# A bidirectional encoder layer with two kinds of attention: 512-column matmuls in the tail, a first attention in blocks of 32 queries, and row sums regrouped by transposes

## The chip, the cores and the metric

The kernel runs on one core of one Trainium2 chip. The metric is the device time of one execution in microseconds (us); lower is better. All times below are of this core.

## The reference

One encoder layer is applied to two sequences of 2048 tokens and 1024 features, with shared weights. All data is float32.

```
h = rms_norm(x, norm_w)
q_a, k_a, v_a, g_a, q_b, k_b, v_b, g_b = split(h @ w_in)     # 512 128 128 512 512 512 512 512
o_a = windowed_gqa_sink(rope(norm(q_a)), rope(norm(k_a)), v_a, sink) * silu(g_a)
o_b = neighbourhood_attn(norm(q_b), norm(k_b), v_b, rpb) * silu(g_b)
x   = x + concat(o_a, o_b) @ w_out
out = x + (p @ w_ple) * sigmoid(x @ w_ple_gate)
```

The first attention (A) has 8 query heads of 64 features on 2 key heads; a token sees the tokens up to 128 away on both sides, and each head has a learned sink in its softmax's denominator. The second attention (B) has 8 heads; the tokens form a grid of 32 rows by 64 columns, and a token sees 8 rows by 16 columns around it, with a learned bias per relative position.

## The kernel before

Every matrix product is made in split precision: an operand is split into a high part (a rounded copy, made on ScalarE) and a low part (the rest, made on VectorE or GpSimd), and three matmuls, high x high, low x high and high x low, add up in PSUM. That is why a matmul appears in threes.

The order of all work is written by a planner in the kernel itself (class `Flow`). Each operation is given an engine, a planned duration, what it depends on, a priority, and the buffers that it takes and frees. `Flow.run` plays the engines through in planned time and emits, on each engine, the ready operation with the lowest priority number. On the chip every engine then runs its own list strictly in that order; a planned duration that is too short shows up as a wait there. All loads and stores are issued by one queue, SyncE's (SP), also in that order. Low-priority projections (`low`, 1000 and up) fill TensorE's time between the attention's steps.

**First attention.** `proj_a` takes 32 tiles of 128 tokens: keys and values in 24 matmuls of 256 columns, queries in 24 of 512, then norms and rotation. `prep_q` transposes a tile's queries and splits them; `unit_a` does the attention for a tile and one key head: `softmax` makes four score blocks, each of 128 queries of one head against 384 keys (256 at a sequence's ends) in two matmuls; VectorE adds the mask and takes the maximum, ScalarE does the exponential, GpSimd divides; twelve transposes, then six matmuls of 512 columns with the values.

**Row regrouping.** B uses the tokens in another order (tiles of 8 rows by 16 columns), so the mean squares of the rows must move from one order to the other. `regroup` runs once per sequence, when its last tile is projected: it writes 2048 values from a tile of 128 partitions by 16 columns to DRAM, each value by itself, writes the roots likewise, and reads the values back in the new order with 16 small loads, one per column.

**Second attention.** 64 steps: two halves of four heads, each of 2 sequences x 16 tiles. `proj_b` makes a tile's queries and keys (24 matmuls of 512 columns) and values (24 of 256, with ScalarE and VectorE writing the split values that are stored to DRAM by window), seven steps ahead of `unit_b`, which does the tile's attention. Beside that, `combine` makes sums of weight blocks on GpSimd for the tail, and after the last projection `embed` makes p @ w_ple in 384 matmuls of 512 columns.

**The tail.** Three stages of products with a 1024 x 1024 weight: the gate paths, the output projection, and the last gate. Each is done by a seven-product (Strassen-Winograd) scheme: per group of 512 tokens, taken as two halves of 256, `operand` builds seven moving operands from the group's quarters by additions and splits them; `product` multiplies each with a 512 x 512 weight set (`a11 a12 s2 s1 s3 a22 s4`), 48 matmuls of 256 columns, into two PSUM banks; `result` evicts a bank when it holds a partial or a final result, with the stage's gate or residual step (VectorE, ScalarE, GpSimd) and its side inputs. Sums of two result blocks share a bank over several products, so some products wait until an earlier result has been read. All seven weight sets of a stage stay in SBUF; the next stage's are loaded and split while the last group runs. Everything the tail needs beyond the first weights takes memory that is given free when the attention's pool (`ab_stack`) is closed, after the last step of B.

All instructions that go through the `Ordered` wrapper appear at line 210 of the profile; the matmuls of projections and attention at line 268, transposes at 271, the tail's matmuls at 1066.

## Time and profile before

| | us |
|---|---|
| median of 3 runs | 2729.1 |
| lowest, highest | 2724.32, 2730.3 |
| the profiled execution | 2731.31 |
| its span, first to last instruction | 2729.5 |

| engine | busy, us | share of the span |
|---|---|---|
| TensorE matmuls (PE) | 2567.4 | 94% |
| TensorE weight loads (PEld) | 2313.6 | 85% |
| VectorE (DVE) | 1949.8 | 71% |
| ScalarE (ACT) | 1549.6 | 57% |
| GpSimd (POOL) | 1462.6 | 54% |

The mean granted TensorE clock is 0.983 of full speed. Matmuls are pipelined: one of 256 columns is shown as busy for 0.28 us while the next begins before it ends, so a busy share near 100% does not say how many matmuls go through. The count of matmuls in a stretch does. A wait is put down to the engine whose signal came last. In a row of a group, the figures behind the bar are busy time, the mean of one in ns, and the idle time of the engine just before these instructions.

### The profile page before, as it was taken

How to read it: one execution, taken by the hardware profiler on the slowest of the kernel's cores; microseconds unless marked ns; L12 is line 12 of the kernel's file. 1: busy time of each engine (PE TensorE's matmuls, PEld its weight loads, DVE VectorE, ACT ScalarE, POOL GpSimd, SP SyncE). 2: the span in 40 equal slices, each digit the busy share in tenths (PEclk: the TensorE clock that was granted, in tenths of full speed). 3: DMA queues.
4: the chain of work that ended last, by engine and by line, in shares of the span. 5: the costliest groups of instructions: out<-in, count | busy, mean ns of one | idle time of the engine just before them, and what ended most of it. 6: DMA issues, size and time to landing. Idle time of an engine off the chain costs nothing. (4 is left out here: it accounts for less than half of the span.)

```text
span 2729.5 us, 49655 instructions
## 1 busy us (share of the span) xinstructions
PE 2567.4 (94%) x17264; PEld 2313.6 (85%) x17264; DVE 1949.8 (71%) x4054; ACT 1549.6 (57%) x3449; POOL 1462.6 (54%) x1517
## 2 busy tenths in 40 slices
PE   7999799989999999999999999899998999999999
PEld 6888688878787877787788777799988999999999
DVE  6888688977777667766767732988888554677775
ACT  6888588867676667766667765433333111243333
POOL 5666466655555554565555532567664232246654
PEclk9999899999999999999999999999999999999999
DMA  4534353335666667667666677555456544654453
GB/s 143 182 106 128 81 158 117 98 76 150 214 215 205 196 202 225 203 203 218 203 208 210 208 250 235 166 180 160 155 171 209 194 161 147 196 172 140 151 177 105
DMA packets 319466, 472.01 MB, mean 173 GB/s; under 512 B 72784, under 2 KB 178384, under 8 KB 309712
## 3 DMA queue, kind: packets, MB, share of 16 engines
q1 hardware_dynamic: 319216, 468.85, 55.2%
q8 instruction: 136, 2.23, 0.4%
q14 instruction: 114, 0.93, 0.1%
HBM read 321.91 MB, written 145.78 MB: 171 GB/s over the span
## 5 line engine op out<-in xcount | busy, mean ns | idle before, releaser
L268 PE MATMUL bank<-wa,xr 128*128 128x256 f32 (+1 forms) x2304 | 413.3, 326 | 14.2 <-DVE mx L210 11.4
L210 POOL TENSOR_SCALAR s<-s,rd 128x384 f32<-128x384 f32 (+4 forms) x512 | 291.1, 587 | 250.9 <-DVE rd L210 118.6
L268 PE MATMUL bank<-wb,xr 128*128 128x512 f32 x1536 | 405.4, 401 | 2.0 <-DVE big L210 1.6
L210 POOL TENSOR_TENSOR xr<-st,xr 128x512 fp32r<-128x512 f32 x208 | 268.2, 1291 | 216.9 <-ACT xr L210 200.1
L268 PEld LDWEIGHTS bank<-wa,xr 128*128 128x128 f32 x2304 | 337.9, 192 | 49.7 <-DVE mx L210 15.8
L210 ACT ACTIVATE s<-s,nm 128x384 f32<-128x384 f32 (+4 forms) x512 | 307.2, 602 | 81.3 <-DVE nm L210 79.3
L268 PEld LDWEIGHTS bank<-wb,xr 128*128 128x128 f32 x1536 | 274.8, 190 | 49.3 <-DVE big L210 1.8
L1066 PE MATMUL bank<-xr,s 128*128 128x256 f32 x2304 | 287.0, 285 | 15.2 <-DVE s L210 10.8
L1066 PEld LDWEIGHTS bank<-xr,s 128*128 128x128 f32 x2304 | 282.5, 194 | 17.0 <-issue 7.7
L210 DVE TENSOR_TENSOR p_t<-bank,p_t 128x512 fp32r<-128x512 f32 (+3 forms) x440 | 263.0, 624 | 41.5 <-ACT p_t L210 38.8
L268 PE MATMUL bank<-big,q 128*128 128x384 f32 (+4 forms) x1024 | 253.3, 355 | 22.3 <-DVE mx L210 8.4
L210 POOL TENSOR_TENSOR y<-vr,half_neg 128x8 f32<-128x8 f32 (+1 forms) x128 | 186.6, 1458 | 136.1 <-DVE vr L210 124.7
L210 ACT CAST p_t<-bank 128x512 fp32r<-128x512 f32 (+3 forms) x440 | 223.9, 541 | 53.5 <-PE bank L271 44.0
L210 DVE TENSOR_TENSOR s<-bank,s 128x512 f32<-128x512 f32 x208 | 142.5, 686 | 146.5 <-PE bank L1066 145.0
L271 PE MATMUL bank<-ident,s 128*128 128x128 f32 (+2 forms) x1568 | 225.1, 277 | 16.9 <-DVE big L210 7.1
L271 PEld LDWEIGHTS bank<-ident,s 128*128 128x128 f32 (+2 forms) x1568 | 181.5, 140 | 50.9 <-issue 13.0
L268 PEld LDWEIGHTS bank<-big,q 128*128 128x128 f32 x1024 | 165.5, 189 | 63.4 <-DVE mx L210 19.1
L210 DVE SCALAR_TENSOR_TENSOR big<-bank,wk,big 64x128 fp32r<-64x128 f32 x320 | 137.6, 430 | 110.2 <-ACT big L210 103.0
L210 DVE TENSOR_TENSOR ot<-bank,ot 64x256 f32<-64x256 f32 (+1 forms) x256 | 141.7, 553 | 85.9 <-ACT ot L210 81.4
L1066 PE MATMUL bank<-xr,wb 128*128 128x256 f32 x1584 | 195.8, 284 | 3.6 <-ACT xr L210 2.8
L1066 PEld LDWEIGHTS bank<-xr,wb 128*128 128x128 f32 x1584 | 193.3, 193 | 4.2 <-ACT xr L210 3.2
L210 ACT COPY ot<-bank 64x256 f32<-64x256 f32 (+1 forms) x256 | 121.4, 474 | 125.5 <-PE bank L268 98.8
(124 smaller groups left out, 5224.5 us busy)
## 6 DMA issues: line engine op xcount, KB each, us to landing
st<-x_b SPq DMA_DIRECT2D x128, 256.0 KB
vw<-v_d SPq DMA_DIRECT2D x107, 256.0 KB
st<-x_a SPq DMA_DIRECT2D x64, 256.0 KB
st<-x_n SPq DMA_DIRECT2D x64, 256.0 KB
v_d<-sq SPq DMA_DIRECT2D x64, 256.0 KB
ple_d<-raw SPq DMA_DIRECT2D x64, 256.0 KB
raw<-x_r SPq DMA_DIRECT2D x16, 1024.0 KB
og_d<-s SPq DMA_DIRECT2D x64, 256.0 KB
```

What stands on the lines that cost most here:

```text
L210: return lambda *a, **k: self.tc.keep_in_program_order(f(*a, **k))
L268: pinned(nc.tensor.matmul(out, lhsT, rhs, start=start, stop=stop))
L271: pinned(nc.tensor.transpose(out, in_, ident))
L1066: pinned(nc.tensor.matmul(ps, w[k][:, x, c:c + 128], o[:, y, k], start=new and kk == 0 and k == 0 and j == 0, stop=k == 3 and j == 2, skip ...
```

## The change

- **Tail.** Groups of 1024 tokens, in two halves of 512. A matmul has 512 columns; a product is 48 of them into four banks. There are 12 groups instead of 24. Operand additions and splits act on 2048 columns instead of 1024, results keep their 512. The fifth product's weight set (`s3`) and the second's (`a12`) share four tiles, so both are loaded and split again in every group. Side inputs go through two tiles.
- **Memory.** Pools are no longer closed; single tiles pass from one use to the next at three points: when the last projection is done, when the embedding is done, when the attention is done.
- **First attention.** A score block has 32 queries of each of the four heads of a key head, against the 288 keys that these can see (fewer at a sequence's ends), instead of 128 queries of one head against 384. The columns outside are set to zero once. Each of the four blocks has its own two tiles. The sink becomes one value per partition, which saves one small VectorE step.
- **Row regrouping.** The values and the roots of a sequence are transposed on TensorE into 32 rows, written to DRAM as rows of 128 values, read back in four loads, put in order by a VectorE copy and transposed back.
- **Second attention.** The values of both halves are projected in the first half, in 24 matmuls of 512 columns per tile, and evicted in two steps. At the beginning and at the turn of the halves, two tiles' query and key projections go ahead of their value projections.
- **Projections** are planned in pieces of two blocks of 128 features (six matmuls) instead of one. The first weights are loaded through four tiles instead of nine. The embedding's results go to tiles that come free with the last projection.

The core of the diff:

```diff
-TW = 256
-NU = SEQ // TW
+NU = 8
...
-    s_pool = pool(SB, [128, 512], F32, "s", mid)
-    p_pool = pool(3, [128, 2, 512], F32R, "p_t", mid, True)
-    x_pool = pool(2, [128, 2, KT, 128], F32R, "xr", mid, True)
-    st_pool = pool(2, [128, 512], F32, "st", mid, True)
-    big = [ap.tile([128, 4096], F32R, tag=f"big{i}", name=f"big{i}") for i in range(3)]
+    s_tiles = [new([128, 512], F32, f"s{i}") for i in range(SB)]
+    s_pool = Pool(s_tiles[8:])
+    s_block = [Pool(s_tiles[2 * b:2 * b + 2]) for b in range(4)]
...
+    first_pool = Pool(qa_pool.tiles)
+    ev_pool = Pool([])
...
+        parts = []
+        for b in range(4):
+            c0, c1 = max(32 * b, 128 * (k0 - t + 1)), min(32 * b + 288, 128 * (k1 - t + 1))
+
+            def sc(bank, b=b, c0=c0, n=c1 - c0):
+                c = 128 * (t - 1) + c0
+                for j, w in enumerate((hi[kv](), q2.t[:, kv])):
+                    mm(bank.t[:, :n], w[:, 128 * b:128 * b + 128], ks_a[:, kv, c:c + n], j == 0, j == 1)
+            parts.append((c1 - c0, sc, lambda b=b, c0=c0, c1=c1: mask[:, c0 - 32 * b:c1 - 32 * b], Slot(s_block[b]), c0))
...
-        vb, vops = project(f, "pv", 256, 120, xs, xdone, w_v, v_done, low(prios[1]), free=[xs])
+        after_pe[f] = (ops[-1], ops[-1])
+        if half:
+            return
+        vb, vops = project(f, "pv", 512, 231, xs, xdone, w_v, v_done, low(prios[1]), free=[xs], chunk=CH)
...
+        for hf in range(2):
+            sv = Slot(sq_pool)
+            v4 = lambda sv=sv: sv.t.bitcast(F32R).rearrange("p (h a d) -> p h a d", a=2, d=HD)
+            vp = lambda hf=hf: vb.t[:, 256 * hf:256 * hf + 256].rearrange("p (h d) -> p h d", d=HD)
+            vpr = pr + 0.1 + 0.2 * hf
...
-        l0 = dma(ms_d[s * SEQ:(s + 1) * SEQ].rearrange("(t p) -> p t", p=128), ms_a[:, c], 8, [root_ops[f] for f in range(NT * s, NT * s + NT)], pr)
-        dma(hr_d[s * SEQ:(s + 1) * SEQ].rearrange("(t p) -> p t", p=128), hr_a[:, c], 8, [root_ops[f] for f in range(NT * s, NT * s + NT)], pr)
-        rows = ms_d.rearrange("(r k c) -> r k c", k=4, c=16)
-        ls = [dma(ms_b[:, i:i + 1], rows[8 * (i // 4):8 * (i // 4) + 8, i % 4, :].rearrange("r c -> c r"), 8, [l0], pr)
-              for i in range(NT * s, NT * s + NT)]
+        bank, back = Slot(banks), Slot(banks)
+        own = [root_ops[f] for f in range(NT * s, NT * s + NT)]
+        t1 = op("PE", 110, lambda: tr(bank.t[:32, :128], mh_a[:, s].rearrange("p a t -> p (a t)")), own, pr, take=[bank])
+        c1 = op("DVE", 150, lambda: V.tensor_copy(out=mt[:32], in_=bank.t[:32, :128]), [t1, *(regrouped[-1:])], pr, free=[bank])
+        l0 = dma(ms_d[s * SEQ:(s + 1) * SEQ].rearrange("(t p) -> t p", p=128), mt[:NT], 8, [c1], pr)
+        l1 = dma(hr_d[s * SEQ:(s + 1) * SEQ].rearrange("(t p) -> t p", p=128), mt[NT:2 * NT], 8, [c1], pr)
+        rows = ms_d[s * SEQ:(s + 1) * SEQ].rearrange("(b r k c) -> b k r c", r=8, k=4, c=16)
+        ls = [dma(mt[4 * b:4 * b + 4].rearrange("k (r c) -> k r c", c=16), rows[b], 8, [l0, l1], pr) for b in range(4)]
+        c2 = op("DVE", 150, lambda: V.tensor_copy(out=mt[32:32 + NT].rearrange("p (c r) -> p c r", r=8),
+                                                  in_=mt[:NT].rearrange("p (r c) -> p c r", c=16)), ls, pr)
+        t2 = op("PE", 110, lambda: pinned(nc.tensor.transpose(back.t[:, :NT], mt[32:32 + NT], ident[32:32 + NT, 32:32 + NT])), [c2], pr, take=[back])
...
-        slot, n = Slot(s_pool), len(parts)
+        slot, n = Slot(first_pool), len(parts)
...
+    w_v, v_done = load_wide(wa, rows_of(w_in_c, 512), True, HB - 9, [after_pe[HB - 1], *ci])
...
+    order = {f: (2 * f, 2 * f + 1) for f in range(HB, 3 * HB)}
+    for f in (HB, 2 * HB - 2):
+        order[f], order[f + 1] = (2 * f, 2 * f + 2), (2 * f + 1, 2 * f + 3)
...
+    sets = {"a11": wa[4:], "a12": wa[:4], "s3": wa[:4]}
+    for i, name in enumerate(("s2", "s1")):
+        sets[name] = [big[i][:, 1024 * j:1024 * j + 1024].rearrange("p (a c) -> p a c", a=2) for j in range(4)]
...
+    def no_projections():
+        for j in range(4, 8):
+            t = new([128, 2, 512], F32R, f"wb{j}", f"vx{j}")
+            give(vw_pool, [t[:, 0], t[:, 1]])
+        for j in range(2):
+            t = new([128, 2, 512], F32, f"wb{j}", f"ev{j}")
+            give(ev_pool, [t[:, 0], t[:, 1]])
+
+    def no_embeddings():
+        sets["s4"] = [new([128, 2, 512], F32R, f"wb{j}", f"s4{j}") for j in range(4)]
+        give(od_pool, [t.rearrange("p a k t -> p (a k t)") for t in x_pool.tiles])
+        give(side_pool, st_pool.tiles)
+
+    def no_attention():
+        sets["a22"] = [new([128, 2, 512], F32R, f"wb{j}", f"a22{j}") for j in range(4, 8)]
+        p2 = new([128, 6, 512], F32, "p_t", "p2")
+        v2 = new([128, 5, 512], F32, "vw", "v2")
+        q3, q4 = new([128, 2048], F32, "q1", "q3"), new([128, 2048], F32, "q2", "q4")
+        o2 = new([128, 2, 2048], F32R, "big2", "o2")
+        give(raw_pool, [q3, q4, p2[:, :4].rearrange(f2), v2[:, :4].rearrange(f2)])
+        give(sum_pool, [misc.rearrange(f2), qb_all.rearrange("p a b c -> p (a b c)")])
+        give(th_pool, [p2[:, 4], p2[:, 5]])
+        give(s_pool, [v2[:, 4]])
+        give(root_pool, sq_pool.tiles)
+        give(od_pool, [o2[:, 0], o2[:, 1]])
...
+    load_q(0, "a11", PR - 13, [after_pe[f][1] for f in (2 * HB - 2, 2 * HB - 1)])
+    for name, gate, pr in (("a12", emb_end, -3), ("s2", att_end, -2), ("s1", att_end, -1), ("a22", att_end, 0), ("s4", emb_end, 1)):
+        load_q(0, name, T0 + pr, [gate])
+    groups = [(stage, g) for stage in range(3) for g in range(4)]
...
+            def go(st=st, mp=mp):
+                w, c = sets[name], 128 * mp
+                o = [x.t.rearrange("p (k t) -> p k t", k=4) for x in (hi, lo)]
+                for k in range(4):
+                    for j, (x, y) in enumerate(((0, 0), (1, 0), (0, 1))):
+                        pinned(nc.tensor.matmul(st[0].t, w[k][:, x, c:c + 128], o[y][:, k], start=first and k == 0 and j == 0,
+                                                stop=k == 3 and j == 2, skip_group_check=True))
+            st[1] = op("PE", 2770, go, [ha, la, *wd, st[1], st[2]], T0 + m + 0.1 * mp, take=[st[0]] if first else (),
+                       free=[hi, lo] if mp == 3 else ())
...
+            m = 7 * n + i
+            if i == 4:
+                load_q(stage, "s3", T0 + m - 2.5, product_ops[m - 3])
+            if i == 1 and n:
+                load_q(stage, "a12", T0 + m - 3.5, product_ops[m - 4])
+            product(m)
+            if g == 3 and stage < 2 and STEPS[i] not in ("a12", "s3"):
+                load_q(stage + 1, STEPS[i], T0 + m + 1, product_ops[m])
...
-    q = np.arange(128)[:, None]
-    k = np.arange(384)[None, :]
+    q = np.arange(128)[:, None] % 32
+    k = np.arange(288)[None, :]
```

More of the change, by code (lines that the diff above doesn't have):

```diff
@@ L214 @@
 AHEAD = 2500
+CH = 2
 KEEP = {"proj": 3, "prep": 2, "sc": 3}
@@ L825, in emit @@
+        v = op("DVE", 300, var, [t2], pr + 1, free=[back])
+        regrouped.append(v)
+        stats_ops[s] = (v, rsqrt(ms_b[:, c], rs_b[:, c], NT, [v], pr + 1))
     sum_ops = {}
```

451 lines of the change are left out of this document (213 added, 238 removed).

## Prediction

> **What bounds the kernel now.** I read the page first, then the busy table by stretches, then stretches of TensorE's and the DMA queue's timelines, then the groups of VectorE in single stretches.
>
> ```profile
> span 2729.5 us, 49655 instructions
> PE 2567.4 (94%) x17264; PEld 2313.6 (85%) x17264; DVE 1949.8 (71%) x4054; ACT 1549.6 (57%) x3449; POOL 1462.6 (54%) x1517
> ...
> PE   7999799989999999999999999899998999999999
> ...
> PEclk9999899999999999999999999999999999999999
> ```
>
> TensorE is busy nearly everywhere; the other engines have room in the mean. But a busy matmul is a pipelined one, so I count matmuls per us instead. The table gives, for each stretch, its length and each engine's busy time with the number of instructions, then granted clock, DMA share and GB/s.
>
> ```profile
> 20.00:250.00 230.00, 220.96 (x1281) 186.96 (x1280) 189.54 (x601) 182.75 (x501) 149.59 (x255) 0.99 0.41 123
> 250.00:340.00 90.00, 74.36 (x411) 62.62 (x411) 62.26 (x198) 59.49 (x166) 48.94 (x79) 0.91 0.47 117
> 340.00:590.00 250.00, 244.71 (x1447) 210.36 (x1446) 219.11 (x682) 208.38 (x564) 169.11 (x284) 1.00 0.39 115
> 590.00:640.00 50.00, 38.61 (x222) 33.31 (x221) 33.12 (x103) 30.69 (x83) 26.07 (x30) 0.90 0.39 75
> ...
> 1150.00:1500.00 350.00, 333.89 (x2006) 281.30 (x2006) 242.31 (x619) 238.00 (x552) 196.62 (x206) 0.99 0.68 209
> ...
> 1691.00:1800.00 109.00, 89.92 (x684) 87.24 (x683) 90.68 (x84) 43.10 (x65) 59.44 (x33) 0.94 0.59 194
> 1800.00:2000.00 200.00, 192.48 (x1583) 190.25 (x1582) 162.21 (x141) 68.50 (x98) 132.87 (x79) 1.00 0.52 160
> 2000.00:2100.00 100.00, 87.58 (x684) 87.00 (x684) 92.94 (x91) 41.45 (x63) 55.63 (x32) 0.93 0.62 205
> 2100.00:2300.00 200.00, 200.00 (x1669) 200.00 (x1668) 101.44 (x117) 35.84 (x35) 60.05 (x25) 1.00 0.51 170
> 2350.00:2450.00 100.00, 94.19 (x759) 93.81 (x758) 74.62 (x76) 40.51 (x60) 42.71 (x20) 0.97 0.58 184
> 2450.00:2700.00 250.00, 250.00 (x2085) 250.00 (x2085) 181.46 (x146) 94.47 (x130) 149.13 (x80) 1.00 0.47 151
> 2700.00:2729.00 29.00, 23.83 (x199) 23.62 (x197) 11.18 (x13) 7.38 (x11) 9.70 (x8) 0.97 0.31 100
> ```
>
> The kernel has three parts: first attention up to about 640, second attention and embedding up to 1691, the tail after that. In the tail 1669 matmuls of 256 columns go in 200 us at clock 1.00, which is 0.1198 us each, and nothing else is visible there: TensorE's own pace is the bound. What 512 columns cost is seen in TensorE's timeline (start, us, what).
>
> ```profile
> 1681.78 9.71 PE L268 MATMUL bank<-xr,wa 128*128 128x512 f32 x42
> ...
> 2103.84 5.92 PE L1066 MATMUL bank<-xr,wa 128*128 128x256 f32 x48
> 2109.61 5.92 PE L1066 MATMUL bank<-xr,wb 128*128 128x256 f32 x48
> ```
>
> Forty-eight of 256 columns go from 2103.84 to 2109.61, 0.120 each, as before. The 42 of 512 columns take 9.71 in all; without the last one's own length, some 0.39, that is 9.32 over 41 steps, 0.2273 each. That is less than twice 0.1198. A straight line through both puts 384 columns at 0.1736 and 288 at 0.1332 (an estimate).
>
> **The tail, where most of it lies.** The tail has 24 groups x 7 products x 48 = 8064 matmuls of 256 columns: 8064 x 0.1198 = 966.1. After, 12 groups x 7 x 48 = 4032 of 512: 4032 x 0.2273 = 916.5. That removes 49.6, all of it on the path.
>
> The tail now lasts 2729.5 - 1691 = 1038.5, so about 72 are not pace. By stretch, length less count x 0.1198: 27.1 at the start (1691 to 1800), 10.4 in 1800 to 2000 (the first stage), 18.1 in 2000 to 2100 (change to the second stage), 9.1 in 2350 to 2450 (change to the third), none in between, some 5.7 at the end.
>
> The start: now every operand tile of the tail waits until the attention's pool is closed. After, tiles pass on one by one, the first weights and the first quarter are loaded earlier, and the embedding goes on beside the loads. Still, three quarters of 1 MB and three sets of weights come only with the attention's end. I take 15 (5 to 27).
>
> The stages turn on VectorE:
>
> ```profile
> L210 DVE TENSOR_TENSOR sum<-sum,raw 128x1024 f32<-128x1024 f32 x15 | 42.1, 2807 | 16.5 <-POOL sum L210 16.5
> ...
> L210 DVE TENSOR_TENSOR sum<-sum,raw 128x1024 f32<-128x1024 f32 x16 | 19.5, 1218 | 0.2
> ...
> L210 DVE TENSOR_TENSOR sum<-sum,raw 128x1024 f32<-128x1024 f32 x72 | 143.0, 1986 | 30.6 <-POOL sum L210 30.3
> ...
> L210 DVE TENSOR_TENSOR wa<-wa x16: 678/684/2829, 1126.8 to 2421.9; 128x512 fp32r<-128x512 f32 x16
> ```
>
> The first row is 1800 to 2000, the second 2100 to 2300, the third the whole run (busy, mean ns, idle before); the last one the split of a weight tile (min, median, max). The same addition takes 2807 ns where GpSimd is 66% busy and 1218 where it is 30% busy. A group of 512 tokens has 336 matmuls, so VectorE works 162.21 x 336 / 1583 = 34.4 on it in the first stage, 68.9 for 1024 tokens. The change adds two weight sets reloaded per group, eight splits of about 1 us (0.68 to 2.83): 77. TensorE's pace for that group is 336 x 0.2273 = 76.4. So in the first stage VectorE is level with TensorE. I take 82 per group (77 if VectorE never waits, 86 if it is 90% busy), against 84.9 now: 4 x 5.6 = 22 of stall. A wait for a bank now has three blocks of 2.7 behind it instead of one of 2.9, which speaks for the lower half. In the third stage the same sum gives 181.46 x 336 / 2085 x 2 + 8 = 66.5, 87% of the pace: I take 1.5 per group, 6 (0 to 14). In the second, 101.44 x 336 / 1669 x 2 + 8 = 48.8: nothing.
>
> The change of stage: its longest stall is behind VectorE.
>
> ```profile
> 2084.52 13.72 PE L1066 MATMUL bank<-xr,s 128*128 128x256 f32 x96 [7.55 <-DVE s L210]
> ```
>
> 28 tiles are split there beside one group of 40; after, 20 beyond the steady eight beside one of 77. I take 8 for 18 and 3 for 9, and 6 at the end. Together 15 + 22 + 8 + 3 + 6 + 6 = 60 for 72. The tail gives 49.6 + 12 = 61.
>
> The reloads themselves I cost at nothing on the path. The fifth product's set shares its tiles with the second's: its four loads wait until that product ends and are needed two products later, 2 x 48 x 0.2273 = 21.8. Four issues, a landing and four splits are some 10 (an estimate from the split's row and the landing below). SyncE waits in order, so the next quarters, side inputs and the stores stand behind that wait. If the cover were gone, each us late costs up to 23 us over the tail.
>
> **First attention.** Scores: 14 inner tiles x 2 sequences x 2 key heads x 8 = 448 matmuls fall from 384 to 288 columns: 448 x 0.0404 = 18 (24 if 288 went at the pace of 256). The 64 of the edge tiles fall from 256 to between 160 and 256 and I give them nothing. VectorE's, ScalarE's and GpSimd's shares of that work shrink by the same quarter, so none of them takes TensorE's place. Transposes and value products stay.
>
> Row regrouping:
>
> ```profile
> 284.55 0.43 SPq L210 DMA_DIRECT2D ms_d<-ms_a  x1
> ...
> 299.91 6.03 SPq L210 DMA_DIRECT2D ms_b<-ms_d  x6
> ...
> 306.16 7.17 PE L268 MATMUL bank<-wa,xr 128*128 128x512 f32 x21 [8.48 <-DVE mx L210]
> ...
> 611.63 1.12 PE L271 MATMUL bank<-ident,raw 128*128 128x128 f32 x4 [11.05 <-POOL raw L210]
> ```
>
> The row sums are written to DRAM four bytes at a time; SyncE's in-order queue can read them back only 15 us later (284.55 to 299.91), and the first six of the sixteen small reads hold it another 6. The attention's copies and the loads of x stand behind, and TensorE idles 8.48 at one sequence, 11.05 at the other. The quiet stretches run (1281 + 1447) / 480 = 5.683 matmuls per us; by that 250 to 340 loses 90 - 411 / 5.683 = 17.7 and 590 to 640 loses 50 - 222 / 5.683 = 10.9, together 28.6 with the lower clock (0.91, 0.90) in it. After, a transpose makes rows of 512 bytes: two writes, four reads, two small copies. The nearest row for such a transfer is the first one of the kernel:
>
> ```profile
> 1.18 0.42 SPq L210 DMA_DIRECT2D wkt<-qk_norms  x1
> ...
> 2.86 0.23 DVE L210 TENSOR_TENSOR wk<-wkt 128x1 f32<-128x1 f32 x2 [2.86 <-DMA wkt<-qk_norms]
> ```
>
> 1.7 from issue to use. Two such waits per sequence, on SyncE and on VectorE, where the first attention's evictions stand behind the copy: I leave 3 per sequence (0 to 8). Gain 28.6 - 6 = 22 (12 to 28).
>
> The start: twelve weight loads now go through nine tiles, then through four that must be split first; I add 2 (0 to 5). First attention: 18 + 22 - 2 = 38.
>
> **Second attention.** The value projection's 64 x 24 = 1536 matmuls of 256 columns become 768 of 512: 1536 x 0.1198 - 768 x 0.2273 = 9.4. But all of them move into the first half of the 64 steps.
>
> ```profile
> L210 DVE TENSOR_TENSOR qb<-bank,y 128x256 f32<-128x256 f32 x24 | 9.9, 415 | 0.0
> L210 DVE SCALAR_TENSOR_TENSOR sq<-bank,rs_b,sq 128x256 fp32r<-128x256 f32 x23 | 11.1, 481 | 7.9 <-ACT sq L210 7.6
> ```
>
> These are of 1150 to 1500: 24 steps in 350, 14.6 each, with VectorE 242.31 / 24 = 10.1 and ScalarE 238.00 / 24 = 9.9. After, a step of the first half has 24 x (0.2273 - 0.1198) = 2.6 more on TensorE, one of the second 24 x 0.1198 = 2.9 less: 17.2 and 11.7, if both stay bound by TensorE. In the second half VectorE then needs 10.1 - 0.48 = 9.6 of 11.7, 82%; in 340 to 590 it was 219.11 of 250, 88%, beside a TensorE at full pace. So I keep the 9.4 and put 25 on both sides. Eight value weight tiles instead of four at the seam to the first attention are hidden by the first two steps' query and key projections, which now go ahead of them; uncovered they are some 5.
>
> The embedding's results go to other tiles, free once the last projection is done:
>
> ```profile
> L268 PE MATMUL bank<-xr,wa x384: 387/389/769, 1558.4 to 1691.1; 128*128 128x512 f32 x192
> ```
>
> It starts only there today too, so this is nothing. Projections ordered in double pieces keep their instructions; an urgent one may wait one piece of 6 x 0.2273 longer, which is within the 25.
>
> **Sum.** 38 + 9 + 61 = 108 or 109. The profiled execution took 2731.31, its span 2729.5; the median of the three runs, 2729.1, is 2.2 below it. 2731.3 - 109 = 2622, less 2.2: 2620.
>
> **Rivals.**
> *VectorE takes the tail over, slower than before.* GpSimd works the same total in a shorter time, so it overlaps VectorE more. If all of VectorE's tail work grew as the addition does from its run's mean to its first-stage mean, 2807 / 1986 = 1.41, a first-stage group takes 77 x 1.41 = 109 and a third-stage one 66.5 x 1.41 = 94: 4 x 27 + 4 x 16 = 172 more, 2792. It decides once the eight groups lose 14 each beyond my forecast, VectorE at about 96 in the first stage. For it: 2807 against 1218. Against: the third stage ran without loss at VectorE 73%. Chance 0.06. The Trainium skill's GPSIMD Engine Reference, in Key points, says that GpSimd shares its SBUF interfaces with VectorE and contends with instructions of two SBUF inputs; the trace agrees.
>
> *The second half is bound by VectorE and ScalarE.* Its steps then stay at 14.6 and the first half pays its 2.6 all the same: 32 x 2.9 = 93 lost, 2713. For it: two engines with nearly 10 of busy time each in 11.7, and many handovers between them. Against: the 88% above. Chance 0.07; with first-stage groups at 86 on top (4 x 4 = 16) it is 2729, even, and I give that 0.03 of the 0.07.
>
> *Wide matmuls bring nothing*, the change not doing what it says: if the tail's 512 columns cost twice 0.1198, the 49.6 are gone, 2670. Against: the 42 in a row at 0.2273, weights and operands of the same kind. Chance 0.05. The Trainium skill's TensorE: Matmul & The Clock Gate, in Back-to-back issue gap, gives N/2.4 + 2.5 ns at full clock: 109 and 216 ns, by which the tail would gain 10.5 and the time be 2659. The trace shows 119.8 and 227.3, and the measurement decides.
>
> *The stalls vanish too.* If tail stalls fall to 15 and the lighter first attention and merged projection save 25 more: 2620 - 45 - 25 = 2550. Chance 0.07.
>
> **How the numbers follow.** The forecast has 0.75. Its own terms, squared together (tail 35, second attention 25, first attention 12), give about 45; with the 2670 case it covers 2570 to 2685. Left out are 2550, 2713 and 2792, together 0.20. Faster by over 0.2% (5.5 us, about what a measurement of this kernel can tell): 0.75 + 0.05 + 0.07 + 0.04 = 0.91; even 0.03; slower 0.06.
>
> **What would show it.** Right: a tail of about 977 with matmuls at 0.227; no idle of 8 us or more at TensorE around 300 and 600; score matmuls 0.13 apart; first-stage groups at 82 with VectorE near 93%. Wrong: VectorE without gaps and TensorE waiting for it throughout the first and third stage; steps of the second half above 13; TensorE waiting for reloaded weights before the second or fifth product of each group.

## The result and the profile after

The changed kernel takes 2706.5 us (median of 4 runs, 2705.06 to 2709.51) beside 2729.1 for the kernel before (2724.32 to 2730.3): a ratio of 0.9922, 95% interval 0.9905 to 0.9939. It is 22.7 us faster; forecast were 109, to 2620 us in a range of 2570 to 2685. The span of the profiled execution went from 2729.5 to 2703.0.

The page of the changed kernel, its head and its slices:

```profile
span 2703.0 us, 39857 instructions
...
PE 2500.4 (93%) x12468; PEld 2053.5 (76%) x12468; DVE 2039.6 (75%) x3950; ACT 1559.5 (58%) x3429; POOL 1433.3 (53%) x1437
...
PE   8999999999999999888888898998887999999998
...
DVE  6888888875567566777777653999989676788887
```

There are 4796 matmuls fewer, and VectorE is busier than before, 2040 us after 1950. TensorE's row has eights where it had nines, in the second half of the second attention and in the tail's first stage; in the latter VectorE stands at nine. The busy table of the changed kernel by stretch (length, then busy time with counts for PE, PEld, DVE, ACT, POOL, then clock, DMA share, GB/s):

```profile
250.00:340.00 90.00, 88.00 (x546) 76.12 (x544) 75.59 (x255) 75.78 (x219) 62.92 (x113) 1.00 0.38 113
...
550.00:600.00 50.00, 47.16 (x250) 38.42 (x249) 41.40 (x114) 35.70 (x90) 28.12 (x38) 1.00 0.41 121
...
1120.00:1500.00 380.00, 329.72 (x1708) 260.83 (x1708) 285.67 (x713) 272.35 (x635) 222.56 (x240) 0.96 0.60 188
1763.00:2040.00 277.00, 245.87 (x1010) 195.72 (x1009) 248.63 (x193) 103.92 (x138) 154.82 (x63) 0.94 0.55 172
2040.00:2147.00 107.00, 82.43 (x336) 66.30 (x335) 84.06 (x68) 27.46 (x33) 38.87 (x14) 0.90 0.53 189
2147.00:2377.00 230.00, 229.42 (x1012) 189.33 (x1011) 170.43 (x149) 61.22 (x57) 72.96 (x16) 1.00 0.62 211
2377.00:2697.00 320.00, 310.55 (x1346) 255.15 (x1344) 266.89 (x187) 133.33 (x174) 193.11 (x82) 0.98 0.53 171
```

The first two rows are where the kernel before stood still at the row regrouping (411 and 222 matmuls, clock 0.91 and 0.90): that is gone. The last four rows are the tail: three first-stage groups, the first group of the second stage, the other three, and the third stage. Where nothing is in the way, 1012 matmuls go in 230 us, 0.2273 each, as forecast. But the three first-stage groups take 277 / 3.006 = 92 us each, with VectorE busy for 90% of it, and the group at the change of stage 107.

Where the time went, part by part. The borders are the first and the last of these two groups, of the kernel before and of the changed one in turn (for each the query eviction of a step; the last embedding matmul was at 1691.1 before):

```profile
L210 DVE TENSOR_TENSOR qb<-bank,y x64: 395/414/422, 618.1 to 1552.7; 128x256 f32<-128x256 f32 x64
```

```profile
L209 DVE TENSOR_TENSOR qb<-bank,y x64: 392/414/426, 573.5 to 1547.5; 128x256 f32<-128x256 f32 x64
```

TensorE's timeline of the changed kernel where the embedding ends (start, length, what):

```profile
1648.35 11.07 PE L1128 MATMUL bank<-o,wa 128*128 128x512 f32 x48
1659.26 21.24 PE L270 MATMUL bank<-xr,wa 128*128 128x512 f32 x93
1687.38 1.22 PE L1128 MATMUL bank<-xr,big 128*128 128x512 f32 x2 [6.88 <-ACT xr L209]
```

The embedding's last matmul starts at 1659.26 + 21.24 - 0.39 = 1680.1. One product of the tail, 48 matmuls worth 10.9 us, already runs ahead of it; the table counts it for the tail.

| part | before | after | change | forecast |
|---|---|---|---|---|
| up to the first step of the second attention | 618.1 | 573.5 | -44.6 | -38 |
| from there to the embedding's end, without the early product | 1073.0 | 1095.7 | +22.7 | -9 |
| the rest, with the early product | 1038.4 | 1033.8 | -4.6 | -61 |

The second row hides two opposite changes. From the first to the last step's queries the changed kernel takes 974.0 us instead of 934.6, 39.4 more; from there to the embedding's end, without the early product, it takes 121.7 instead of 138.4, 16.7 less.

### The profile page after: what moved, and what is told of

It is laid out like the page before. It is cut to its first block, busy times and chain, and to the rows that moved or that the text cites. A ratio compares the mean times of both kernels' runs of the same rounds, so it can differ in the third digit from the quotient of the medians.

```text
span 2703.0 us, 39857 instructions
## 1 busy us (share of the span) xinstructions
PE 2500.4 (93%) x12468; PEld 2053.5 (76%) x12468; DVE 2039.6 (75%) x3950; ACT 1559.5 (58%) x3429; POOL 1433.3 (53%) x1437
## 5 line engine op out<-in xcount | busy, mean ns | idle before, releaser
L270 PE MATMUL bank<-wa,xr 128*128 128x512 f32 x1536 | 388.7, 397 | 6.6 <-DVE wa L209 2.0
L209 POOL TENSOR_SCALAR s<-s,rd 128x288 f32<-128x288 f32 (+6 forms) x512 | 271.8, 550 | 228.9 <-DVE rd L209 154.9
L209 ACT ACTIVATE s<-s,nm 128x288 f32<-128x288 f32 (+6 forms) x512 | 288.2, 565 | 89.4 <-DVE nm L209 88.0
L270 PE MATMUL bank<-big,q 128*128 128x288 f32 (+4 forms) x1024 | 238.2, 345 | 24.2 <-DVE mx L209 9.7
L1128 PE MATMUL bank<-o,wa 128*128 128x512 f32 x912 | 212.7, 392 | 6.4 <-DVE o L209 6.2
L1128 PE MATMUL bank<-xr,wa 128*128 128x512 f32 x816 | 196.3, 400 | 19.2 <-DVE xr L209 10.3
L1128 PEld LDWEIGHTS bank<-o,wa 128*128 128x128 f32 x912 | 172.0, 189 | 44.0 <-DVE o L209 7.5
L1128 PEld LDWEIGHTS bank<-xr,wa 128*128 128x128 f32 x816 | 157.1, 193 | 56.0 <-DVE xr L209 11.7
L209 ACT COPY misc<-bank 64x256 f32<-64x256 f32 (+1 forms) x256 | 121.3, 474 | 129.5 <-PE bank L270 100.1
L209 DVE TENSOR_TENSOR misc<-bank,misc 64x256 f32<-64x256 f32 (+1 forms) x256 | 141.7, 554 | 68.0 <-ACT misc L209 63.6
```

Of the source, the lines that this page charges most:

```text
L209: return lambda *a, **k: self.tc.keep_in_program_order(f(*a, **k))
L270: pinned(nc.tensor.matmul(out, lhsT, rhs, start=start, stop=stop))
L1128: pinned(nc.tensor.matmul(st[0].t, w[k][:, x, c:c + 128], o[y][:, k], start=first and k == 0 and j == 0, stop=k == 3 and j == 2, skip_grou ...
```

## Experiments

Theory after the result: the tail's first stage and its change of stage are held by VectorE, which GpSimd's simultaneous work stretches and which the reloaded weight sets load further; the second attention lost through the values moved into its first half. Rivals: the planned order, not an engine's capacity, makes TensorE wait in the tail; the reload costs through the queue and not through its splits; the second half only lacks filler. Each ratio is to the kernel before on the same chip. The lengths of steps and groups in the text are the time between the first and the last `qb<-bank,y` of a half, divided by 31, and between the starts of every 336th tail matmul of the trace.

### The row regrouping alone

The kernel before, with only the new `regroup` and its tiles:

```diff
+        t1 = op("PE", 110, lambda: tr(bank.t[:32, :128], mh_a[:, s].rearrange("p a t -> p (a t)")), own, pr, take=[bank])
+        c1 = op("DVE", 150, lambda: V.tensor_copy(out=mt[:32], in_=bank.t[:32, :128]), [t1, *(regrouped[-1:])], pr, free=[bank])
```

> The kernel before with the new row regrouping alone. Theory (the four-byte writes hold the DMA queue and idle TensorE): the two idle stretches of 8 and 11 us around 300 and 600 vanish and the time falls by 20 to 28, to about 2705. Rival (the first attention's gain in the changed kernel came from the smaller scores, the queue was covered): under 6 us, 2723 or more.

Measured: 2706.6, ratio 0.9916 (0.99 to 0.9933). The regrouping gives what it was forecast to give, and that is as much as the whole change gives. Its second attention begins at 592.5, that of the changed kernel at 573.5: the other 19.0 are what the rest of the change gives up to there, with the scores against 288 columns (forecast 18) as its largest part and the start against it; no run separates these two. The score matmuls follow each other by 0.133 us (median), as forecast.

### Values by half again

```diff
-        if half:
-            return
-        vb, vops = project(f, "pv", 512, 231, xs, xdone, w_v, v_done, low(prios[1]), free=[xs], chunk=CH)
+        vb, vops = project(f, "pv", 256, 120, xs, xdone, w_v, v_done, low(prios[1]), free=[xs], chunk=CH)
```

> The changed kernel with the value projection of each half done in that half again, 24 matmuls of 256 columns per step. Theory (without value projections to fill TensorE between the attention's steps, the second half's steps take 13.3 for 9.9 of TensorE work, while the first half's grow in full): steps of 14.6 in both halves, 32 x (16.9 + 13.3 - 29.2) = 32 less and 2 us either way, about 2674. Rival (steps are slower for another reason, such as the larger pieces or the memory): both halves stay slow, within 10 of 2706.

The edit also loads the value weights half by half again, and the tail's first weight set later.

Measured: 2691.7, ratio 0.9865 (0.9844 to 0.9885): 0.57% or 15.6 us better than the changed kernel, about half of what was expected. Steps are 15.0 and 15.2 us long, where the kernel with the regrouping alone has 14.5 and 14.8. So the merge is one cause, and there is another.

### Single pieces

`CH = 2` becomes `CH = 1`, once in the changed kernel and once together with the values by half.

> The changed kernel, with the projections queued in single pieces again (one eighth of a projection for each piece, as in the kernel before) instead of double ones. Theory A: the 23 us that the second attention still loses with the value projections back in their own half come from the double pieces, which hold urgent transposes and scores back for up to 1.4 us: about 2686 us. Theory B (that of the prediction): the pieces are worth nothing, and the loss lies in the rest of the merge: 2703 to 2709 us.

> The changed kernel, with the value projection by half (256 columns in each half) and the projections in single pieces: both edits of the second attention undone. If the two are the whole loss there, its steps are 14.6 us long as in the kernel before and the time is about 2668 us. If something else of the change slows the second attention (the order of the score slots, the fewer result tiles), it stays near 2690 us.

Measured: 2701.5, ratio 0.9889 (0.9874 to 0.9905), and 2682.3, ratio 0.9819 (0.9804 to 0.9833). With values by half, the single pieces are worth 0.46%, 12.6 us, and the queries of the 64 steps are through at 1508.9 after a first one at 575.1: 933.8 us, where the kernel with the regrouping alone needs 935.5. The two edits are the whole loss in the steps of the second attention. In the changed kernel itself, the pieces are worth 0.33%, with intervals that touch. The 933.8 are 40 less than the changed kernel's 974.0, but the kernel gained only 28. Where the rest went is seen in the stretch between the last step's queries and the end of the attention's last seven units, here of the kernel with both edits undone:

```profile
1509.00:1578.00 69.00, 53.35 (x290) 44.53 (x289) 47.90 (x122) 48.88 (x119) 30.29 (x42) 0.85 0.64 197
```

and of the changed kernel:

```profile
1547.50:1640.40 92.90, 87.89 (x482) 73.52 (x481) 48.87 (x130) 70.04 (x159) 34.05 (x45) 1.00 0.67 219
```

In the changed kernel the embedding's matmuls run between those of the last units, TensorE is full, the clock 1.00. With both edits undone the embedding comes behind the attention: it was queued behind the last weight sums on GpSimd (`sum_ops[2]`).

### The embedding, as filler of the second half, and early

First the changed kernel, with the embedding spread over the second half:

```diff
-                prev = op("PE", 693, go, [done[k], *p_done, prev, *sum_ops[2][-1:]], 5003.5 + 0.1 * b + 0.01 * m, take=[bank, ev] if k == 0 else (),
+                prev = op("PE", 693, go, [done[k], *p_done, prev], low(2 * gate + m + 1.5), take=[bank, ev] if k == 0 else (),
...
+        if f >= 2 * HB + 1 and (f - 2 * HB - 1) % 4 == 0:
+            embed((f - 2 * HB - 1) // 4, w_p, p_done, f - 5.4, f)
```

> The changed kernel, with the embedding's 384 matmuls taken out of the stretch behind the last projection and queued as filler between the projections of the second half of the second attention (its weights come in as soon as the last value projection is done). Theory A: the second half of the changed kernel has too little projection work to fill TensorE (9.9 us of matmul work in a step of 13.3 us), so the 87 us of embedding fits in its gaps: about 40 us less than the changed kernel, 2667 us. Theory B: the steps of the second half are bound by VectorE, ScalarE and the hand-overs between them, and filler lengthens each step by nearly its own length: 2695 to 2710 us.

The edit also gives the embedding other tiles and loads the tail's first weight set only behind it.

Measured: 2731.8, ratio 0.9998 (0.9987 to 1.0009), 21 us slower than the changed kernel and slower than either theory expected. The steps of the second half grew from 13.55 to 15.73 us, by 2.18 for 384 x 0.2273 / 32 = 2.73 us of filler in each. So four fifths of the filler lengthen the step: the second half was not merely short of matmuls. The filler is not TensorE's alone, though: its evictions and copies raise ScalarE's busy time per step from 9.7 to 10.9 us, and the run does not tell the two apart. And the last units then stand without any:

```profile
1619.00:1692.60 73.60, 56.65 (x299) 44.48 (x297) 53.88 (x131) 53.79 (x126) 25.21 (x35) 0.93 0.51 153
```

The attention ends some 51 us later than in the changed kernel (its last store is issued at 1692.6 instead of 1641.2), and the tail waits for it.

Then the kernel with both edits undone, and the embedding only freed from the weight sums, `[done[k], *p_done, prev]`, so that it comes right after the last projection:

> The kernel with both edits of the second attention undone (values by half, single pieces), and the embedding no longer queued behind the last weight sums, which its operands do not need. In that kernel the first embedding result is stored 60 us after the last projection, in the changed kernel about then. Theory A: the embedding is the filler of the attention's last seven units, and moving it back there ends it 30 us sooner: 2652 us. Theory B: the last units slow down by as much as is filled in: 2675 to 2682 us.

Measured: 2678.3, ratio 0.9812 (0.9797 to 0.9828); not to be told from the 0.9819 without the edit. The embedding's last store is indeed issued at 1649.7 instead of 1676.5, but the attention's last units now end at 1623 instead of 1578, and the tail's start needs both. Theory B's time comes out, its reason only in part: in the profiled executions the tail's first group still ends 15 us sooner (1737.0 instead of 1752.3), and the next four groups lose 10 of these again (382.6 instead of 372.5); why, no run shows.

### No reload, a reload without splits, and ready-made halves

Three edits of the reloaded sets `a12` and `s3`. The first loads them only in the first group of a stage (the later products of these two steps use the wrong set); the second loads them each time but leaves out the splitting after the first; the third stores both halves once and reloads them ready made.

```diff
-            if i == 4:
+            if i == 4 and g == 0:
...
+            if again:
+                w_done[i, name].append(ld)
+                continue
...
+        w_done[i, name] = [dma(lambda j=j: sets[name][j].bitcast(F32), kept[i, name][j].rearrange("a p c -> p a c"), 512,
+                               [*deps, kept_ops[i, name][j]], prio) for j in range(4)]
```

> The changed kernel without reloading and splitting the two shared weight sets after the first group of each stage (the second or the fifth product then uses the other's weights). Theory (the first stage is bound by VectorE): each of three first-stage groups loses eight splits of about 1.3 us, 30 to 45 in all, with 0 to 10 in the third stage, so 2655 to 2676. Rival (operands and results come late by the planned order, not by VectorE's load): under 10, 2696 or more.

> The changed kernel, with the two shared weight sets loaded for every group as there, but not split again after the first group of a stage (leaves the splitting out, so those products use wrong weights). Theory A: the eight copies and eight subtractions are what the reload costs: as without any reload, 30 us less than the changed kernel, about 2680 us. Theory B: the reload costs through SyncE's wait for the earlier product and the landing of the loads: as the changed kernel, 2700 to 2710 us.

> The changed kernel, with the two weight sets that are reloaded for every group split only once in a stage: both halves are then stored, and the later groups load both halves ready made, so each group has eight copies on ScalarE and eight subtractions on VectorE less and twice the bytes of these loads. Theory A: the reload costs through the splits (about 10 us of VectorE in each group of the first stage): 25 us less than the changed kernel, 2681 us. Theory B: it costs through the wait of SyncE's queue and the landing of the loads, which are longer now: 2706 us or more.

Measured: 2676.8, ratio 0.9814 (0.9791 to 0.9837); 2697.9, ratio 0.9882 (0.9867 to 0.9897); 2733.5, ratio 1.0005 (0.9992 to 1.0017). The reload costs 1.08%, 29 us. Without its splits only 0.40%, 11 us, come back, in the first stage (9 us) and the second (7), while the third is 5 longer; the other 18 stay with the loads. Of those, 14 lie in the third stage, 324.7 us with the loads alone and 310.7 without. Here the third stage of the kernel that loads but does not split:

```profile
2363.30:2688.00 324.70, 312.21 (x1344) 255.67 (x1344) 227.53 (x163) 121.13 (x150) 187.50 (x82) 0.98 0.53 169
```

and of the one without reload:

```profile
2355.30:2666.00 310.70, 306.04 (x1344) 251.60 (x1343) 241.46 (x158) 121.60 (x150) 201.56 (x81) 1.00 0.47 154
```

VectorE has no more to do in the slower one (227.53 against 241.46), so there it is not its load. TensorE waits longest for an operand that GpSimd splits, once in each of the last three groups. The first of these waits with the loads, and the same one without:

```profile
2465.57 12.33 PE L1131 MATMUL bank<-o,big 128*128 128x512 f32 x46 [3.69 <-POOL o L209]
```

```profile
2455.34 10.73 PE L1128 MATMUL bank<-o,big 128*128 128x512 f32 x46 [1.55 <-POOL o L209]
```

With the loads these waits are 3.5 to 3.7 us instead of 1.6, two more of 0.7 follow, and the 46 matmuls behind the long ones take 12.2 to 13.4 us instead of 10.7. Together that is 13 of the 14. In all three groups VectorE's addition for that operand takes 4.7 to 4.9 us, beside GpSimd's next addition on 2048 columns; without the loads it takes 3.4, ahead of that addition. So the loads cost there by the order in which the two engines meet; what in the loads (their place on the one queue, or their landing) changes that order was not separated.

Ready-made halves double the bytes of the reloads: the first stage gains 7 us, the second and third lose 11 and 24. But the loss lies in the first two groups of a stage, of which the first stores the halves: 113.5 and 82.7 us instead of 107.3 and 77.4 in the second stage, 87.7 and 91.3 instead of 76.2 and 80.8 in the third. In the first group of the third stage TensorE waits three times for a tile of the shared set:

```profile
2431.32 0.96 PE L1141 MATMUL bank<-xr,wa 128*128 128x512 f32 x3 [4.03 <-DVE wa L209]
```

The later groups, which reload ready-made halves like the second, take 82.2 and 82.2 instead of 79.2 and 83.6 in the third stage, and in the first stage two of them are 4 to 5 us shorter. So this run does not show that the transfers cost more than the splits; it mixes them with the storing.

### GpSimd's gate product

The changed kernel without GpSimd's product of gate and attention in the first stage (the gate is left out of the result):

```diff
-            o = op("POOL", 1600, gate, [y, ld], pr, free=[side])
+            o = op("NOP", 0, lambda: None, [y, ld], pr, free=[side])
```

> The changed kernel without GpSimd's multiplication by the attention's output in the tail's first stage (the gate path is stored alone). Theory (GpSimd stretches VectorE's instructions with two SBUF inputs): the multiplication by the root falls from 1.40 to below 0.9 us, the one after tanh from 1.20 to below 0.85, and first-stage groups from about 94 to 82 or less, 40 to 55 in all. Rival (those durations have another cause): they stay above 1.1, and the time changes by under 15.

Measured in a single execution: 2646.8, beside a median of 2729.4 for the kernel before on that chip; some 60 us less than the changed kernel. No VectorE operation was taken away. The groups of VectorE in three first-stage groups of the changed kernel (busy, mean ns, idle before):

```profile
L209 DVE SCALAR_TENSOR_TENSOR s<-p,s 128x512 f32<-128x512 f32 x42 | 52.9, 1265 | 6.2 <-ACT p L209 6.2
L209 DVE TENSOR_TENSOR s<-s,sq 128x512 f32<-128x512 f32 x34 | 47.9, 1412 | 0.6
L209 DVE TENSOR_TENSOR wa<-wa 128x512 fp32r<-128x512 f32 x25 | 34.4, 1405 | 8.4 <-ACT wa L209 8.4
L209 DVE TENSOR_TENSOR s<-bank,s 128x512 f32<-128x512 f32 x34 | 22.9, 679 | 4.9 <-PE bank L1128 4.9
```

and in those of the kernel without gate product:

```profile
L209 DVE SCALAR_TENSOR_TENSOR s<-p,s 128x512 f32<-128x512 f32 x44 | 49.0, 1126 | 5.8 <-ACT p L209 5.8
L209 DVE TENSOR_TENSOR s<-s,sq 128x512 f32<-128x512 f32 x35 | 31.5, 908 | 0.5
L209 DVE TENSOR_TENSOR s<-bank,s 128x512 f32<-128x512 f32 x33 | 22.2, 680 | 11.4 <-PE bank L1128 11.4
L209 DVE TENSOR_TENSOR wa<-wa 128x512 fp32r<-128x512 f32 x27 | 17.9, 682 | 0.0
```

The same 512 columns take 1265 to 1412 ns or 680. The one kind that is 679 in both reads a PSUM bank and one SBUF tile; the others read two SBUF tiles. That is the rule of the Trainium skill's GPSIMD Engine Reference, Key points: GpSimd shares its SBUF interfaces with VectorE, and VectorE's instructions with two SBUF inputs contend. The traces agree; the page gives no size, and here it is up to a factor of two in the mean.

Of the theory's two signs one came and one did not: the multiplication by the root (`s<-s,sq`) fell from 1412 to 908 ns, but the one after tanh (`s<-p,s`) only from 1265 to 1126, where below 850 was expected. GpSimd's operations on 2048 columns are still there. The groups fell to 81.2, 80.4 and 84.6 us, the change of stage from 107.3 to 82.7.

### SiLU on ScalarE, and the gate product on VectorE

```diff
-            a = op("ACT", 540, lambda: A.activation(th.t, rt.t, AF.Tanh), [z], pr, take=[th])
-            y = op("DVE", 612, lambda: V.scalar_tensor_tensor(out=rt.t, in0=th.t, scalar=1.0, in1=rt.t, op0=ALU.add, op1=ALU.mult),
-                   [a], pr, free=[th])
+            y = op("ACT", 540, lambda: A.activation(rt.t, rt.t, AF.Silu, scale=2.0), [z], pr)
```

> The changed kernel, with one ScalarE SiLU in the first stage of the tail in place of the tanh and the VectorE operation that multiplies by 1 + tanh: 16 VectorE operations of 1.25 us less in each group of 1024 tokens, GpSimd's gate product stays. Theory A: VectorE's busy time sets the pace of a first-stage group (92.4 us), so the groups fall to about 78 us and the change of stage behind them from 107 to about 92: 55 us less than the changed kernel, 2652 us. Theory B: GpSimd's gate products (1.7 us each, 27 us in a group) and the chain bank, ScalarE, VectorE, GpSimd set it, and VectorE only waits beside them: 10 us less, about 2697 us.

The second run takes this and moves the gate product to VectorE, so that VectorE's count is as in the changed kernel:

```diff
-            o = op("POOL", 1600, gate, [y, ld], pr, free=[side])
+            o = op("DVE", 612, gate, [y, ld], pr, free=[side])
```

> The changed kernel with the SiLU of the first stage on ScalarE, and the gate product moved from GpSimd to the place on VectorE that this frees: VectorE has as many operations in a first-stage group as in the changed kernel, GpSimd only those on 2048 columns. Theory A: VectorE's operations are stretched by GpSimd's that run at the same time (1.2 to 1.4 us instead of 0.68), so without the gate products on GpSimd they take about half, the groups fall to about 80 us and the change of stage to 83: 30 us less than with the SiLU alone, 2650 us. Theory B: the number of VectorE's operations sets the pace, whatever GpSimd does: 2700 to 2710 us, as the changed kernel.

Measured: 2682.3, ratio 0.9829 (0.9801 to 0.9856), and 2660.0, ratio 0.9744 (0.9728 to 0.9761). Sixteen VectorE operations less in each group gave 25 us, half of the 55 expected; with as many as before, but away from GpSimd's products, it is 49, 22 more than with the SiLU alone where 30 were forecast. Three first-stage groups of the run with SiLU alone:

```profile
1757.60:2021.60 264.00, 240.93 (x1009) 194.84 (x1009) 214.90 (x145) 106.53 (x141) 168.29 (x65) 0.95 0.59 189
```

and of the one with the gate on VectorE:

```profile
1761.40:2017.70 256.30, 240.37 (x1010) 194.67 (x1009) 221.76 (x201) 107.82 (x143) 82.17 (x15) 0.96 0.59 189
```

GpSimd works 82.17 instead of 168.29 us there, and VectorE needs only 7 us more for 56 operations more. So neither the number of operations nor GpSimd's own time sets the pace alone; the pair of engines does. The rival that the chain from a bank through the results is too long fits less: TensorE's waits for operands that VectorE makes fall from 11.5 us in the three groups of the changed kernel to 0.9 here, while those that end with one of VectorE's results grow from 4.9 to 9.2.

### The plan with measured costs

The changed kernel, with the tail's planned VectorE costs as the profile has them (2.9 instead of 2.2 us for 2048 columns, 1.2 for a split, 1.3 for the gate's operations):

```diff
-            return op(eng, 2205 if eng == "DVE" else 5100,
+            return op(eng, 2900 if eng == "DVE" else 5100,
```

> The changed kernel, with the tail's VectorE costs in the plan as the profile of the changed kernel shows them (2048 columns 2.9 us instead of 2.2, a split 1.2 instead of 0.6, the two operations of the gate 1.3 instead of 0.6); the work is the same, only the written-out order differs. Theory A: the first stage lacks VectorE time, which no order gives back: 2703 to 2712 us. Theory B: the order, made for an engine twice as fast, is what leaves TensorE waiting: first-stage groups at about 85 us, 2675 us.

Measured: 2699.5, ratio 0.9889 (0.987 to 0.9907), at best 9 us less. The first-stage groups stay where they were (94.0, 90.4, 95.5); the change of stage falls from 107.3 to 91.0, and one group of the second stage and the third stage give all of these 16 us back (87.3 instead of 76.2; 324.5 instead of 319.3). For the first stage theory A holds. At the change of stage the order moves the wait to other groups and does not remove it.

### What works, together

Values by half, single pieces and the early embedding, with the SiLU, and then also with the gate product on VectorE; all edits are shown above.

> The kernel before this one (values by half, single pieces, embedding early) and the SiLU of the first stage together. If the two gains are in different stretches they add: 2652 - 55 = 2597 us. If the start of the tail only moves the wait from the embedding to the attention's end or to the loads of the first group, 20 to 30 us of the first are lost: about 2625 us.

> Values by half, single pieces, embedding early, SiLU, and the gate product on VectorE, all in one. If the gate's move gives the same as in the run before, 2651 - 30 = 2620 us.

Measured: 2650.9, ratio 0.971 (0.9694 to 0.9726), and 2626.6, ratio 0.962 (0.9606 to 0.9634). The first is slower than both of its forecasts, which had counted on 2652 for the early embedding and 55 for the SiLU; these pieces themselves gave 2678.3 and 25. The measured gains of the second attention and of the tail add up; the last version is 3.8% faster than the kernel before and 80 us faster than the changed one.

## Why the prediction was wrong, point by point

**The pace of wide matmuls: right.** 0.2273 us in the tail, with the plain count of 1012 in 230 us. The rival by which they bring nothing fell.

**First attention: right.** -44.6 for -38: the regrouping 25.6 up to this point (22.8 of the whole time) for 22, the rest 19 for 16.

**The tail's first stage: the terms "77" and "82 per group" were too small.** The mechanism was the one forecast, VectorE level with TensorE, and so was the 90% up to which it gets busy. But it was mis-sized twice. VectorE's work in a group is 248.63 x 336 / 1010 = 82.7 us, not 77: the forecast took each operation at its mean length of before, and some became longer. In the first stage before (1800 to 2000) the two result operations with two SBUF inputs were

```profile
L210 DVE SCALAR_TENSOR_TENSOR s<-th,s 128x512 f32<-128x512 f32 x35 | 35.4, 1011 | 16.7 <-ACT th L210 16.7
L210 DVE TENSOR_TENSOR s<-s,root 128x512 f32<-128x512 f32 x27 | 21.3, 787 | 0.6
```

and after the change they take 1265 and 1412 ns, and a split 1405 where about 1000 was put in. That GpSimd works in a shorter time, as the first rival says, is not the reason: it is busy for 154.82 / 277 = 56% of these groups, after 66% before. Which instructions of the two engines meet has changed; what changed it, no run separates. And it was given 82 when the busy share that the forecast itself allowed, 90%, makes 82.7 / 0.90 = 92 of it. Three groups lost 277.1 - 246 = 31 us, and the first rival, put at 0.06, came part of the way: VectorE came to 82.7 where that rival decides at 96.

**The change of stage: the "8 for 18" was wrong.** Stalls there came to 107.3 - 76.4 = 31. TensorE's timeline of the changed kernel:

```profile
2029.77 10.59 PE L1128 MATMUL bank<-o,s 128*128 128x512 f32 x46
2040.20 0.61 PE L1128 MATMUL bank<-xr,wa 128*128 128x512 f32 x2
2048.44 12.37 PE L1128 MATMUL bank<-xr,wa 128*128 128x512 f32 x46 [7.63 <-DVE xr L209]
...
2073.42 11.07 PE L1128 MATMUL bank<-xr,big 128*128 128x512 f32 x48
2095.61 13.09 PE L1128 MATMUL bank<-o,big 128*128 128x512 f32 x48 [11.12 <-DVE s L209]
```

and VectorE's ahead of the second wait's end:

```profile
2077.08 6.79 DVE L209 TENSOR_TENSOR s<-s 128x512 fp32r<-128x512 f32 x2
2083.79 0.68 DVE L209 TENSOR_TENSOR s<-bank,s 128x512 f32<-128x512 f32 x1
2084.39 2.77 DVE L209 TENSOR_TENSOR o<-qb,o 128x2048 fp32r<-128x2048 f32 x1
2087.08 5.58 DVE L209 TENSOR_TENSOR s<-s 128x512 fp32r<-128x512 f32 x2
2092.58 2.28 DVE L209 TENSOR_TENSOR qb<-q,raw 128x2048 f32<-128x2048 f32 x1
2094.79 0.68 DVE L209 TENSOR_TENSOR s<-bank,s 128x512 f32<-128x512 f32 x1
```

TensorE waits 7.63 us for an operand. The 11.12 end with the eviction of a result (`s<-bank,s`, 2094.79 to 2095.46), which stands on VectorE behind four splits of weight tiles (`s<-s`), 12.4 us for what is 0.68 each where GpSimd is quiet. The forecast counted the splits and put a longer group beside them; it did not see that VectorE carries over the backlog of a full first stage, nor that the splits stretch here. Without GpSimd's gate products the same group takes 82.7.

**The reloads at "nothing on the path": wrong, 29 us.** The forecast named the risk (late weights, and the queue behind the waiting issue) and trusted a cover of 21.8 us. The cover nearly held: in the tail TensorE waits for a tile of a shared set 1.74 us once in the first stage, 4.2 at the change of stage and 0.2 behind it. What cost were the splits (11 us, shown by leaving them out) and what hangs on the loads (18 us, 14 of them in the third stage, through an operand that VectorE and GpSimd finish later; why the loads cause that is open).

**Second attention: -9 turned into +23.** The forecast was 17.2 us for a step of the first half and 11.7 in the second; measured are 16.8 and 13.55. The failed step is "if both stay bound by TensorE". The two runs with single pieces show it cleanly: with values by half the steps are 14.33 and 15.04 us long, with merged values 16.93 and 13.42. The first half pays all of its 2.6 us, the second gets back 1.6 of its 2.9. The prediction's own sign of being wrong, steps of the second half above 13, came true. That is the second rival in part, but not by capacity, since VectorE is busy for 285.67 / 380 = 75% there and ScalarE for 72%. That the hand-overs between the engines set the rest is argued, not shown. And "within the 25" for the double pieces held as a bound, but 5 to 13 us of the kernel's time were in it (4.9 us of the steps in the changed kernel, 12.6 of the time with values by half). "So this is nothing" for the embedding was wrong to the good side: it fills TensorE beside the last units, and the stretch behind the steps got 16.7 shorter.

**The start and the third stage: right.** From the embedding's end to the end of the first group it is 1763.1 - 1680.1 = 83 us, forecast 76.4 less the early product's 10.9, plus 15 and 5.6, 86. The third stage took 319.3, forecast 305.6 + 9.

In sum the misses are 31 (groups), 31 - 8 = 23 (change of stage) and 23 + 9 = 32 (second attention), 86 us. Between the forecast -109 and the -26.5 of the two spans lie 82; the first attention's 7 and the start's 3 went the other way, and the third stage took some 5 more. The reloads' 29 are no further term: they lie within these.

## What to carry to other kernels

Before you widen a step so that the leading engine gets shorter, work out the second engine's load at the new pace and divide it by the share that it can really be busy, here 0.90; "level with" means that the second engine leads. When VectorE and GpSimd both work on SBUF tiles, count them as one pair: taking an operation off GpSimd can bring more than taking one off VectorE, and an operation with a PSUM input escapes. And put filler where nothing else is left to do (here the last units of the attention), not where it only adds to a chain.

## What the runs showed of the hardware

VectorE's stretch is an overlap with single GpSimd instructions, not a general slowness. VectorE's timeline of the changed kernel,

```profile
1845.21 5.69 DVE L209 TENSOR_TENSOR wa<-wa 128x512 fp32r<-128x512 f32 x2
1850.83 0.68 DVE L209 TENSOR_TENSOR s<-s,sq 128x512 f32<-128x512 f32 x1
1851.43 0.68 DVE L209 TENSOR_TENSOR wa<-wa 128x512 fp32r<-128x512 f32 x1
```

and GpSimd's:

```profile
1843.10 6.66 POOL L209 TENSOR_TENSOR qb<-q,p 128x2048 f32<-128x2048 f32 x1
```

Of the two splits the first takes 5.09 us, to 1850.3, half a us behind the end of GpSimd's operation on 2048 columns; the second and those behind it take 0.68. The count over the three first-stage groups says the same: of the three kinds with two SBUF inputs above, the 44 instructions beside which no GpSimd instruction runs take at most 694 ns, the 56 others 1.6 to 2.3 us in the mean of a kind. The kind with a PSUM input has GpSimd beside it in 26 of 34 and still takes at most 692. Not every overlap stretches: in the kernel without gate product nine splits run beside GpSimd and take 682 in the mean. Over 1760 to 2040 the splits' row (min, median, max in ns) shows both kinds:

```profile
L209 DVE TENSOR_TENSOR wa<-wa x28: 676/679/5092, 1760.3 to 2004.4; 128x512 fp32r<-128x512 f32 x28
```

A mean over such a mixture, which the forecast used, says little about what a new overlap costs.

A stall costs more than its length. After the waits of 7.63 and 11.12 us above, 46 and 48 matmuls took 12.37 and 13.09 us, where 46 and 48 took 10.59 and 11.07 before them; that is 1.8 and 2.0 us more. The busy table around the two restarts (granted clock third from the end):

```profile
2045.20:2051.90 6.70, 3.46 (x8) 2.79 (x9) 6.67 (x8) 3.02 (x6) 1.63 (x1) 0.50 0.30 78
2089.50:2099.70 10.20, 4.09 (x10) 3.29 (x11) 10.20 (x8) 0.00 (x0) 2.01 (x1) 0.50 0.95 352
```

The clock is at half until 2051.9 and 2099.7 (from 2052 to 2089 it is 1.00), so the matmuls that restart at 2048.44 and 2095.61 run at half pace for 3.5 and 4.1 us. Half of that is about 1.7 and 2.0, the whole of the extra time. In the third stage 46 matmuls behind a wait of 2.24 us took 10.72 us, behind one of 2.79 us 12.30.
